# The low-rank first factors of the decay and the rate, taken from h and h shifted by one token, with the mixing vectors multiplied into the weights

## The chip, the cores and the metric

The kernel runs on one core of a Trainium2 chip. The metric is device time in microseconds (us) of one launch; lower is better. The core's engines work side by side, each through its own list of instructions in order: TensorE (PE in the profile, its weight loads PEld), VectorE (DVE), ScalarE (ACT), GpSimd (POOL), and SyncE (SP), which issues most of the DMAs. They wait for one another through semaphores.

## The reference

Two layers over 512 tokens of width 1024, in float32. Layer 0 is an RWKV-7 time mix and a SwiGLU FFN, layer 1 differential attention and an FFN. The change touches the time mix, which begins so (its scan over tokens and the rest of the model are left out):

```python
h_prev = jnp.pad(h, ((0, 0), (1, 0), (0, 0)))[:, :-1]
hh = h_prev - h
xr = h + hh * mu[0]
xw = h + hh * mu[1]
xk = h + hh * mu[2]
xv = h + hh * mu[3]
xa = h + hh * mu[4]
xg = h + hh * mu[5]
r = xr @ w_r
w = -jax.nn.softplus(-(w0 + jnp.tanh(xw @ w1) @ w2)) - 0.5
k = xk @ w_k
v = xv @ w_v
a = jax.nn.sigmoid(a0 + (xa @ a1) @ a2)
g = jax.nn.sigmoid(xg @ g1) @ g2
...
decay = jnp.exp(-jnp.exp(heads(w)))
```

`h` is the RMS-normalised input. `w1` and `a1` are 1024x64, `w2` and `a2` 64x1024, `w_r`, `w_k` and `w_v` 1024x1024.

## The kernel before, in words

Activations lie with features on the 128 partitions and the 512 tokens along the free dimension: eight tiles of 128 features make the width of 1024 (`KT` = 8; `kt` counts them). Precision comes from splitting a float32 operand into a rounded part (`hi`, type fp32r) and a rest (`lo`). `mm3` (lines 154 to 158) then makes one product of three fp32r matmuls (hi·hi, hi·lo, lo·hi). A plain float32 matmul stands in the trace as two instructions.

**The order.** Program order is written by generators, and a scheduler of the framework then sets the order on each engine. `merge` (line 99) deals out the steps of several generators in proportion to the numbers beside them. The first merge (line 480) has four: `normed` (eight steps that scale the input to h, line 452), two calls of `lora` (the first factors of decay and rate, tags `ca` and `cb`), and `r_half(0)`, the first half of r. After it come `rates` for half 0 (both second factors) and `k_half(0)`. Then `plan` (line 495) runs three streams: the recurrence's preparation and scan for heads 0 to 7, the remaining projections, and the same preparation for heads 8 to 15.

**A mix.** `mix_tile` (lines 366 to 374) makes one 128x512 tile of xr, xw and so on: ScalarE multiplies h by 1-mu (line 372), VectorE adds mu times h shifted by one token (line 373). Its default buffers are tag `xm`, of which there are two.

**Before the change.** `lora` loads a first factor twice side by side (line 381, so the 128 columns of the weight are w1 and w1 again), mixes a tile, and makes one float32 matmul of it per `kt` (line 392). `proj_p` (lines 187 to 206) makes r and k of half 0: per `kt` a mix, its cast to hi (line 199) and its rest (line 200), and twelve fp32r matmuls into four PSUM banks (tag `pj`); every second `kt` also a 512 KB weight load, its cast (line 195) and its rest (line 196). `lora2` multiplies the second factor: since the first result stands twice on the partitions, upper half as hi and lower half as lo (`halves`), a matmul over 128 rows (line 414) and one over 64 rows (line 415) make up the three products. `rates` calls it for decay and rate, eight banks per half, each evacuated by a sigmoid on ScalarE (line 538).

**Buffers** that matter: `wr` 3 (weights as loaded), `xm` 2, `xk` 9 (the mixes of k, kept for both halves), `pr` 7, `z` 6 (hi/lo pairs of `proj_p`), `s` 13, `pj` 4 banks, `ca` and `cb` 2 banks each.

**The end of a scan step.** `head_out` (line 879) normalises 128 tokens of eight heads, then turns them into feature order: four TensorE transposes into one bank (line 911), each followed by its ScalarE evacuation (line 912).

The functions that the change touches:

Of the kernel before, what the change touches and what calls it, by code (L numbers as in the profile page):

```python
# [34 lines left out]
VI = {n: i for i, n in enumerate(VECS)}  # L35
# [7 lines left out]
class Trunk:  # L43
# [3 lines left out]
                 gate=(172, 190, 1.0), out0=(190.5, 252.922016661, 1.25), pairs1=(65, 130, 1.0), solve1=(132.962208526, 188.90025602, 1.0))  # L47


    START = 8, 7.5, 7.5, 8  # L50


    RW = dict(s=13, z=6, b=2, xk=9, xm=2, pr=7, nv=3, it=1, u=2, rs=9, ho=4, ev=1, iv=1)
# [339 lines left out]
            yield  # L393
        out(*pss)

    def halves(self, dst, src):

        nc = self.nc
        nc.scalar.copy(dst, src)
        nc.vector.tensor_tensor(out=dst[C:P], in0=src[C:P], in1=dst[C:P].bitcast(F32), op=ALU.subtract)  # L400

    def lora2(self, x, W2, w, evac):

        nc = self.nc
        raw = self.T("wr", [P, 512])
        for f in (slice(0, C), slice(C, P)):
            nc.sync.dma_start(raw[f], W2[:, w * 512:w * 512 + 512])
        hi, lo = self.T("ho", [P, 512], F32R), self.T("ho", [P, 512], F32R)
        nc.scalar.copy(hi, raw)
        nc.vector.tensor_tensor(out=lo[0:C], in0=raw[0:C], in1=hi[0:C].bitcast(F32), op=ALU.subtract)  # L410
        for i in range(4):
            ps = self.bank()
            c = slice(i * P, i * P + P)
            nc.tensor.matmul(ps, hi[:, c], x, start=True, stop=False)
            nc.tensor.matmul(ps, lo[0:C, c], x[0:C], start=False, stop=True)
            evac(w * 4 + i, ps)

    def gate2(self, pg, w, evac):

# [18 lines left out]
    def rwkv(self, turn):  # L438
        nc, A = self.nc, self.A
# [7 lines left out]
        h = xT  # L447

        def normed():
            for j in range(KT):  # L450
                v = h[j // 2][:, j % 2, :]
                nc.vector.scalar_tensor_tensor(out=v, in0=v, scalar=self.vec("g_mix0", j), in1=bc, op0=ALU.mult, op1=ALU.mult)
                yield
# [4 lines left out]
        for p in range(NP):  # L458
            nc.vector.tensor_scalar(self.rkc[:, p, :], self.cst[:, C_BO:C_BO + 2], self.vec("r_k", p), None, op0=ALU.mult)
        self.lw = cp.tile([P, D], F32, name="lw")  # L460
        nc.sync.dma_start(self.lw, A["lnx_w"].broadcast_to([P, D]))
        self.v_d = self.dr.tile([2, 2, S, 4, C], F32, name="v_d")
        self.st_d = self.dr.tile([2, NCH, P, 4, 8 * C], F32, name="st_d")
        self.sel = cp.tile([P, NT, P], F32, name="sel")
        nc.gpsimd.dma_start(self.sel, A["sel"])
        self.R, self.Pt, self.kept = {}, {}, {}
        self.oT = {}

        pwa = []

        def low(i):
            def out(ps):
                pwa or pwa.append(self.T("s", [P, 2, S], F32R))
                if i:
                    return self.halves(pwa[0][:, 1, :], ps)
                t = self.T("pr", [P, S])
                nc.scalar.activation(t, ps, AF.Tanh)
                self.halves(pwa[0][:, 0, :], t)
            return out
        self.merge(*zip((normed(), self.lora(h, 1, [(A["w1"], 2)], low(0), "ca"), self.lora(h, 4, [(A["a1"], 2)], low(1), "cb"), self.r_half(0)),  # L480
                        self.START))
        sg, aa = self.rates(pwa[0], 0)
        kr, ld, pg, sa, x1 = ([], []), ([], []), [], [(sg, aa)], []
        self.drain(self.k_half(0, kr[0]))

        def rates():
            sa.append(self.rates(pwa[0], 1))
            yield

        def out(w):  # L490
# [3 lines left out]
        t = self.TIMES  # L494
# [12 lines left out]
    def mixes(self, key, m, w):  # L507

        kept = self.kept.setdefault(key, {})

        def mix(kt):
            if key == "r":
                return self.mix_tile(self.h, m, kt)
            if w:
                return kept.pop(kt)
            x = kept[kt] = self.mix_tile(self.h, m, kt, "xk")
            return x
        return mix
# [11 lines left out]
                nc.vector.tensor_tensor(out=lo[g], in0=v[g], in1=hi[g].bitcast(F32), op=ALU.subtract)  # L530
        return self.lora(self.h, 5, [(self.A["g1a"], 1), (self.A["g1b"], 3)], out, "pj")

    def rates(self, low, w):
        nc, A = self.nc, self.A
        sg = [self.T("s", [P, 2, S]) for _ in range(2)]
        aa = [self.T("s", [P, 2, S]) for _ in range(2)]
        for i, W2, dst, b in ((0, A["w2"], sg, "w0"), (1, A["a2"], aa, "a0")):
            self.lora2(low[:, i, :], W2, w, lambda o, ps: nc.scalar.activation(dst[o // 2 - 2 * w][:, o % 2, :], ps, AF.Sigmoid, bias=self.vec(b, o)))
        return sg, aa

    def r_half(self, w):
# [337 lines left out]
    def head_out(self, w, tt, y):  # L879
        nc = self.nc  # L880
# [21 lines left out]
        yo = sq.rearrange("p (a b) c -> p a b c", b=2)  # L902
# [4 lines left out]
        yield  # L907
        ps = self.bank("cb")
        for i in range(4):
            p = w4 + i  # L910
            nc.tensor.transpose(ps[:, i * P:(i + 1) * P], yo[:, i].rearrange("p a b -> p (a b)"), self.ident)
            nc.scalar.activation(self.oT[p // 2][:, p % 2, tt * P:(tt + 1) * P], ps[:, i * P:(i + 1) * P], AF.Identity, bias=self.vec("lnx_b", p))

    def ffn(self, xT, l, tag, out=None):
# [367 lines left out]
```

## Time and profile before

| | us |
|---|---|
| median of 3 runs | 1524.42 (1516.05 to 1524.76) |
| the profiled execution | 1518.63 |
| its span, first to last instruction | 1516.8 |
| PE busy | 1447.9 (95%) |
| VectorE busy | 787.3 (52%) |
| ScalarE busy | 529.1 (35%) |
| GpSimd busy | 187.3 (12%) |

The span has four parts: the load and normalisation of the input (to about 28 us), the time mix (to about 507 us), the first FFN and the attention, and the second FFN. A busy PE is not a PE at its peak: matmuls overlap, so the busy time of one is longer than the distance from one start to the next, and the latter is what a stream of them costs. The granted clock (PEclk) is that of TensorE, 1.00 being 2.4 GHz and 0.50 being 1.2 GHz.

### The profile page before, as it was taken

What the parts mean: (1) busy time and instruction counts of PE and PEld (TensorE: products, weight loads), DVE (VectorE), ACT (ScalarE), POOL (GpSimd) and SP (SyncE); (2) the same over time, 40 slices, a digit from 0 to 9 for tenths busy, and PEclk for the clock granted to TensorE, in tenths of its full rate; (3) what the DMA queues carried; (4) which work ended last, traced back from release to release, by engine and by line L of the source; (5) the groups of instructions that cost most, each with busy time, mean ns of one, the idle gap of its engine ahead of it and who ended that gap; (6) DMA issues with size and microseconds to landing.
All of it is one profiled execution on the core that took longest, in us unless ns stands there. A gap on an engine that the chain in (4) does not pass through costs nothing.

```text
span 1516.8 us, 23107 instructions
## 1 busy us (share of the span) xinstructions
PE 1447.9 (95%) x9576; PEld 1140.0 (75%) x9576; DVE 787.3 (52%) x1511; ACT 529.1 (35%) x926; POOL 187.3 (12%) x156
## 2 busy tenths in 40 slices
PE   3899999999997999999999989999999999999998
PEld 2465555767685788888888879988778888888887
DVE  6735549677666644433323276666665444443222
ACT  4652341213423433222222153556654323232111
POOL 0002313100000111111100023111001111111000
PEclk9989999999998999999999999999999999999999
DMA  5112423776321322222222222111112232322231
GB/s 159 57 69 93 165 105 107 281 241 207 133 89 42 116 96 85 98 97 97 96 93 96 95 92 84 59 68 43 42 43 97 96 99 92 102 91 100 98 122 64
DMA packets 59162, 155.82 MB, mean 103 GB/s; under 512 B 12848, under 2 KB 19248, under 8 KB 57008
## 3 DMA queue, kind: packets, MB, share of 16 engines
q1 hardware_dynamic: 57856, 152.76, 29.3%
q8 instruction: 75, 1.23, 0.3%
q10 hardware_dynamic: 1120, 1.32, 0.3%
q14 instruction: 31, 0.25, 0.1%
q0 software_dynamic: 80, 0.26, 0.0%
HBM read 133.34 MB, written 20.97 MB: 102 GB/s over the span
## 4 chain that ended last, share of the span: by engine, by line
PE 83%; DVE 9%; ACT 3%; POOL 2%; issue 1%; DMA 1%; ACTq 0%; POOLq 0%
PE pj L156 15%; PE pj L157 15%; PE pj L158 15%; PE pj L182 3%; PE pj L216 3%; PE d L1058 2%; PE cb L875 2%; PE d L1060 2%; PE d L1059 2%; PE ca L833 2%; PE cb L743 1%; PE a L1156 1%; PE ca L157 1%; PE cb L157 1%; PE ca L158 1%
## 5 line engine op out<-in xcount | busy, mean ns | idle before, releaser
L150 ACT CAST wh<-wr 128x1024 fp32r<-128x1024 f32 x153 | 160.8, 1051 | 498.4 <-PE pj L157 224.2
L151 DVE TENSOR_TENSOR wl<-wr,wh 128x1024 fp32r<-128x1024 f32 x153 | 187.0, 1223 | 183.7 <-ACT wh L150 182.0
L156 PE MATMUL pj<-xa,wh 128*128 128x512 f32 x352 | 139.2, 395 | 1.3 <-ACT wh L150 1.3
L157 PE MATMUL pj<-xa,wh 128*128 128x512 f32 x352 | 138.9, 395 | 0.0
L158 PE MATMUL pj<-xa,wl 128*128 128x512 f32 x352 | 138.8, 395 | 0.0
L156 PE MATMUL pj<-xb,wh 128*128 128x512 f32 x352 | 137.1, 389 | 0.0
L158 PE MATMUL pj<-xb,wl 128*128 128x512 f32 x352 | 137.0, 389 | 0.0
L157 PE MATMUL pj<-xb,wh 128*128 128x512 f32 x352 | 137.0, 389 | 0.0
L945 POOL TENSOR_TENSOR hid<-ev,hid 128x512 fp32r<-128x512 f32 x44 | 68.2, 1551 | 403.6 <-ACT hid L944 403.6
L941 DVE TENSOR_TENSOR ev<-pj,bc 128x512 f32<-128x512 f32 x44 | 30.4, 691 | 144.5 <-PE pj L158 144.5
L938 DVE TENSOR_TENSOR ev<-pj,bc 128x512 f32<-128x512 f32 x44 | 30.4, 692 | 117.0 <-PE pj L158 114.7
L156 PEld LDWEIGHTS pj<-xa,wh 128*128 128x128 f32 x352 | 66.3, 188 | 17.4 <-ACT wh L150 2.2
L158 PEld LDWEIGHTS pj<-xa,wl 128*128 128x128 f32 x352 | 66.3, 188 | 15.7
L157 PEld LDWEIGHTS pj<-xa,wh 128*128 128x128 f32 x352 | 66.3, 188 | 15.3
L157 PEld LDWEIGHTS pj<-xb,wh 128*128 128x128 f32 x352 | 66.1, 188 | 13.8
L156 PEld LDWEIGHTS pj<-xb,wh 128*128 128x128 f32 x352 | 66.1, 188 | 13.7
L158 PEld LDWEIGHTS pj<-xb,wl 128*128 128x128 f32 x352 | 66.1, 188 | 13.6
L158 PE MATMUL pj<-hid,wl 128*128 128x512 f32 x176 | 68.5, 389 | 0.0
L156 PE MATMUL pj<-hid,wh 128*128 128x512 f32 x176 | 68.5, 389 | 0.0
L157 PE MATMUL pj<-hid,wh 128*128 128x512 f32 x176 | 68.5, 389 | 0.0
L216 PE MATMUL pj<-wr,xk 128*128 128x512 f32 x128 | 63.5, 635 | 0.0
L227 POOL TENSOR_TENSOR ty<-ty,mhalf 128x8 f32<-128x8 f32 (+1 forms) x20 | 35.4, 1770 | 157.6 <-DVE ty L1094 125.7
(337 smaller groups left out, 3124.7 us busy)
## 6 DMA issues: line engine op xcount, KB each, us to landing
wr<-in_wgu SPq DMA_DIRECT2D x88, 512.0 KB, 3.5
wr<-in_wdn SPq DMA_DIRECT2D x44, 512.0 KB, 3.5
st_d<-z SPq DMA_DIRECT2D x16, 1024.0 KB, 4.7
z<-st_d SPq DMA_DIRECT2D x16, 1024.0 KB, 6.3
wr<-in_w_kv SPq DMA_DIRECT2D x16, 512.0 KB, 3.6
wr<-in_w_r SPq DMA_DIRECT2D x8, 512.0 KB, 3.5
wr<-in_w_k SPq DMA_DIRECT2D x8, 512.0 KB, 3.5
wr<-in_w_v SPq DMA_DIRECT2D x8, 512.0 KB, 3.8
```

The source lines that it names most:

```text
L150: nc.scalar.copy(hi, raw)
L151: nc.vector.tensor_tensor(out=lo, in0=raw, in1=hi.bitcast(F32), op=ALU.subtract)
L156: mm(out, wh, xh, start=start, stop=False)
L157: mm(out, wh, xl, start=False, stop=False)
L158: mm(out, wl, xh, start=False, stop=stop)
L182: self.nc.tensor.matmul(pss[i], w[:, kt % 2, i * P:i * P + P], x, start=kt == kts[0], stop=kt == kts[-1])
L216: self.nc.tensor.matmul(pss[tt], x[:, tt * P:(tt + 1) * P], w[:, kt % 2, :], start=kt == 0, stop=kt == KT - 1)
L227: nc.gpsimd.tensor_tensor(out=y, in0=m, in1=half.to_broadcast(shp), op=ALU.pow)
L833: nc.tensor.matmul(ps[f, i * C:(i + 1) * C], L(f, i), R[f, i, :], start=False, stop=n == len(parts) - 1 and i == 3)
L938: nc.vector.tensor_tensor(out=a, in0=pss[0], in1=bc, op=ALU.mult)
L941: nc.vector.tensor_tensor(out=b, in0=pss[1], in1=bc, op=ALU.mult)
L945: nc.gpsimd.tensor_tensor(out=t[:, 1, :], in0=b, in1=t[:, 0, :].bitcast(F32), op=ALU.subtract)
```

## The change

The two `lora` calls become one generator, `lora_h`, and the mixes of decay and rate go away. Since xw = (1-mu)·h + mu·h_prev, xw·w1 equals h·((1-mu)·w1) + h_prev·(mu·w1): the kernel loads w1 and a1 once each, side by side (64 columns each), multiplies both by 1-mu and by mu (four VectorE instructions on 128x8x64), and makes two float32 matmuls per `kt`, one of h and one of h shifted by a token (511 columns), into one bank for both. Rows 0 to 63 of the result are the decay's, 64 to 127 the rate's; Tanh runs on the first, a copy on the second, then one split makes hi and lo. `rates` loads w2 and a2 into the two halves of one tile, splits it once, and uses `mm3` over 64 rows: three matmuls for a bank instead of two. "Three changes" are also: r's mixes of half 0 use the seven `pr` buffers instead of the two `xm`; the loads of `lw` and `sel` stand later in the program; and `head_out` makes its four transposes ahead of the four evacuations.

```diff
-    START = 8, 7.5, 7.5, 8
+    START = 8, 7.5, 8
...
-    def halves(self, dst, src):
...
-    def lora2(self, x, W2, w, evac):
...
-        for i in range(4):
-            ps = self.bank()
-            c = slice(i * P, i * P + P)
-            nc.tensor.matmul(ps, hi[:, c], x, start=True, stop=False)
-            nc.tensor.matmul(ps, lo[0:C, c], x[0:C], start=False, stop=True)
-            evac(w * 4 + i, ps)
+    def lora_h(self, h, tag):
+        nc, A = self.nc, self.A
+        raw = self.T("wr", [P, KT, P])
+        W = [self.T("s", [P, KT, P]) for _ in range(2)]
+        for i, (m, n) in enumerate(((1, "w1"), (4, "a1"))):
+            c = slice(i * C, i * C + C)
+            nc.sync.dma_start(raw[:, :, c], A[n])
+            j = VI[f"mu{m}"] * KT
+            for t, f in zip(W, (self.omu[:, m * KT:(m + 1) * KT], self.par[:, j:j + KT])):
+                nc.vector.tensor_tensor(out=t[:, :, c], in0=raw[:, :, c], in1=f.unsqueeze(2).to_broadcast([P, KT, C]), op=ALU.mult)
+        ps = self.bank(tag)
+        mm = nc.tensor.matmul
+        for kt in range(KT):
+            x = h[kt // 2][:, kt % 2, :]
+            now = lambda: mm(ps, W[0][:, kt, :], x, start=kt == 0, stop=kt == KT - 1)
+            if kt == 0:
+                now()
+            mm(ps[:, 1:S], W[1][:, kt, :], x[:, 0:S - 1], start=False, stop=False)
+            if kt:
+                now()
+            yield
+        t = self.T("pr", [P, S])
+        nc.scalar.activation(t[0:C], ps[0:C], AF.Tanh)
+        nc.vector.tensor_copy(t[C:P], ps[C:P])
+        self.low = self.T("s", [P, 2, S], F32R)
+        nc.scalar.copy(self.low[:, 0, :], t)
+        nc.vector.tensor_tensor(out=self.low[:, 1, :], in0=t, in1=self.low[:, 0, :].bitcast(F32), op=ALU.subtract)
...
-        self.merge(*zip((normed(), self.lora(h, 1, [(A["w1"], 2)], low(0), "ca"), self.lora(h, 4, [(A["a1"], 2)], low(1), "cb"), self.r_half(0)),
-                        self.START))
-        sg, aa = self.rates(pwa[0], 0)
+        self.merge(*zip((normed(), self.lora_h(h, "ca"), self.r_half(0)), self.START))
+        sg, aa = self.rates(0)
...
-                return self.mix_tile(self.h, m, kt)
+                return self.mix_tile(self.h, m, kt, "xm" if w else "pr")
...
-    def rates(self, low, w):
+    def rates(self, w):
...
+        raw = self.T("wr", [P, 512])
+        F = slice(0, C), slice(C, P)
+        for f, n in zip(F, ("w2", "a2")):
+            nc.sync.dma_start(raw[f], A[n][:, w * 512:w * 512 + 512])
+        hi, lo = self.T("ho", [P, 512], F32R), self.T("ho", [P, 512], F32R)
+        nc.scalar.copy(hi, raw)
+        nc.vector.tensor_tensor(out=lo, in0=raw, in1=hi.bitcast(F32), op=ALU.subtract)
+        for f, dst, b in zip(F, (sg, aa), ("w0", "a0")):
+            for i in range(4):
+                ps = self.bank()
+                c = slice(i * P, i * P + P)
+                self.mm3(ps, hi[f, c], lo[f, c], self.low[f, 0, :], self.low[f, 1, :], True, True)
+                nc.scalar.activation(dst[i // 2][:, i % 2, :], ps, AF.Sigmoid, bias=self.vec(b, w * 4 + i))
...
         for i in range(4):
+            nc.tensor.transpose(ps[:, i * P:(i + 1) * P], yo[:, i].rearrange("p a b -> p (a b)"), self.ident)
+        for i in range(4):
             p = w4 + i
-            nc.tensor.transpose(ps[:, i * P:(i + 1) * P], yo[:, i].rearrange("p a b -> p (a b)"), self.ident)
             nc.scalar.activation(self.oT[p // 2][:, p % 2, tt * P:(tt + 1) * P], ps[:, i * P:(i + 1) * P], AF.Identity, bias=self.vec("lnx_b", p))
```

Outside the time mix the order on the engines stays. In it, the scheduler's order moves at three places that matter below. The first is VectorE at the end of the input's norm, from the reciprocal root (its last steps write `rstd`; `ty` are small tiles) to the first scaling of x into h. Before:

```order
L229 TENSOR_TENSOR ty_127<-ty_125 128x4
L979 SCALAR_TENSOR_TENSOR hcol<-hcol,cst 128x1
L230 SCALAR_TENSOR_TENSOR ty_127<-ty_127,ty_122 128x4
L231 SCALAR_TENSOR_TENSOR rstd_124<-ty_127,ty_125 128x4
L1000 TENSOR_SCALAR sgn<-sgn 128x1
L253 TENSOR_SCALAR pr_132<-cst,rstd_124 128x128
```

Now, with `s_192` and `s_193` the two weight tiles of `lora_h` and `wr_191` the loaded w1 and a1:

```order
L229 TENSOR_TENSOR ty_127<-ty_125 128x4
L407 TENSOR_TENSOR s_192<-wr_191,omu 128x8x64
L230 SCALAR_TENSOR_TENSOR ty_127<-ty_127,ty_122 128x4
L407 TENSOR_TENSOR s_193<-wr_191,par 128x8x64
L231 SCALAR_TENSOR_TENSOR rstd_124<-ty_127,ty_125 128x4
L407 TENSOR_TENSOR s_192<-wr_191,omu 128x8x64
L253 TENSOR_SCALAR pr_132<-cst,rstd_124 128x128
L407 TENSOR_TENSOR s_193<-wr_191,par 128x8x64
```

Three of the four weight multiplications stand between the steps of the reciprocal root, in place of one-column instructions that move behind them; the fourth stands behind the instructions of line 253.

The second is ScalarE from the last evacuation of r to the sigmoids (`pr` takes Tanh's output, `s_413` and `s_368` the split first factor, `z` the pairs of k). Before:

```order
L545 COPY s_164<-pj_169 128x512
L199 CAST z_479<-xk_482 128x512
L477 ACTIVATE pr_414<-ca_196 128x512
L199 CAST z_479<-xk_499 128x512
L399 CAST s_413<-pr_414 128x512
L399 CAST s_413<-cb_204 128x512
L195 CAST z_518<-wr_516 128x1024
L538 ACT_TABLE_LOAD
```

Now:

```order
L553 COPY s_162<-pj_167 128x512
L195 CAST z_511<-wr_509 128x1024
L199 CAST z_512<-xk_515 128x512
L420 ACTIVATE pr_365<-ca_200 64x512
L199 CAST z_512<-xk_532 128x512
L423 CAST s_368<-pr_365 128x512
L546 ACT_TABLE_LOAD
```

A 128x1024 weight cast moves from behind the split to a place ahead of Tanh. On VectorE the subtraction that ends the split (line 424) stands behind line 196 of the same pair, the copy of the rate's rows (line 421) and two instructions of line 200.

The third is PE at the same point. Before, the last two first-factor matmuls are followed by `lora2`'s pairs of a 128-row and a 64-row matmul:

```order
L392 MATMUL ca_196<-xm_405,wr_193 128x512
L392 MATMUL cb_204<-xm_409,wr_201 128x512
L414 MATMUL pj_431<-s_413,ho_427 128x512
L415 MATMUL pj_431<-s_413,ho_428 128x512
L414 MATMUL pj_435<-s_413,ho_427 128x512
```

Now:

```order
L415 MATMUL ca_200<-x_70,s_193 128x511
L412 MATMUL ca_200<-x_70,s_192 128x512
L156 MATMUL pj_382<-s_368,ho_378 128x512
L156 MATMUL pj_387<-s_368,ho_378 128x512
L156 MATMUL pj_392<-s_368,ho_378 128x512
L156 MATMUL pj_397<-s_368,ho_378 128x512
L157 MATMUL pj_382<-s_368,ho_378 128x512
L158 MATMUL pj_382<-s_368,ho_379 128x512
```

The first-factor matmuls read the tiles of h themselves, and all 24 matmuls of the second factors are over 64 rows, twelve on rows 0 to 63 and then twelve on rows 64 to 127. At the start of the stage three of the sixteen first-factor matmuls stand ahead of r's first.

On SP, w1 and a1 are each issued once instead of twice, the second w_r load follows them at once, and `lw` stands behind that; w2 and a2 are issued once each.

## Rows read from the trace of the kernel before

**Rows 1.** Busy time by stretch. The columns are the stretch and its length in us, then for PE, PEld, DVE, ACT and POOL busy us and (x instructions), the granted clock, the DMA share and GB/s.

```profile
9.00:13.40 4.40, 0.00 (x0) 0.00 (x0) 2.55 (x5) 1.20 (x3) 0.00 (x0) 1.00 1.03 355
...
41.00:75.40 34.40, 28.61 (x96) 17.51 (x96) 23.90 (x34) 21.22 (x34) 0.00 (x0) 1.00 0.19 59
77.40:80.40 3.00, 2.95 (x7) 1.29 (x7) 1.92 (x2) 2.97 (x5) 0.00 (x0) 1.00 0.63 253
80.40:90.50 10.10, 10.10 (x19) 5.33 (x19) 2.08 (x3) 6.89 (x12) 0.00 (x0) 0.51 0.13 50
```

**Rows 2.** Timeline of PE in two rounds of that stage: start us, busy us (modelled, longer than the distance to the next start), instruction; in brackets idle time before it.

```profile
61.26 1.02 PE L392 MATMUL ca<-xm,wr 128*128 128x512 f32 x2
62.12 1.02 PE L392 MATMUL cb<-xm,wr 128*128 128x512 f32 x2
64.53 1.19 PE L156 MATMUL pj<-z,z 128*128 128x512 f32 x4 [1.39 <-ACT z L199]
65.56 0.39 PE L157 MATMUL pj<-z,z 128*128 128x512 f32 x1
65.79 0.39 PE L158 MATMUL pj<-z,z 128*128 128x512 f32 x1
70.68 1.19 PE L156 MATMUL pj<-z,z 128*128 128x512 f32 x4 [1.39 <-ACT z L199]
```

**Rows 3.** Groups of instructions by line from 28.5 to 75.4 us: busy us, mean ns of one, idle before.

```profile
L373 DVE SCALAR_TENSOR_TENSOR xm<-x,par,xm 128x511 f32<-128x511 f32 x22 | 16.4, 749 | 9.0 <-ACT xm L372 8.5
L372 ACT ACTIVATE xm<-x,omu 128x512 f32<-128x512 f32 x22 | 15.8, 720 | 13.5 <-PE ca L392 10.6 <-DVE z L200 1.5 <-PE cb L392 0.7
L199 ACT CAST z<-xm 128x512 fp32r<-128x512 f32 x8 | 4.9, 616 | 1.1 <-DVE xm L373 1.1
L200 DVE TENSOR_TENSOR z<-xm,z 128x512 fp32r<-128x512 f32 x8 | 5.5, 684 | 0.0
L156 PEld LDWEIGHTS pj<-z,z 128*128 128x128 f32 x32 | 6.0, 201 | 13.6 <-ACT z L199 11.7 <-issue 1.0
```

**Rows 4.** Timeline of VectorE in the input's norm.

```profile
13.35 0.69 DVE L265 TENSOR_TENSOR pr<-x 128x512 f32<-128x512 f32 x1 [1.60 <-DMA x<-in_xT]
...
25.07 1.41 DVE L452 SCALAR_TENSOR_TENSOR x<-x,par,cb 128x512 f32<-128x512 f32 x2 [1.58 <-PE cb L254]
```

**Rows 5.** DMA issues of SP in the first 30 us: start us, us in the queue, number of issues.

```profile
13.34 1.37 SPq L381 DMA_DIRECT2D wr<-in_a  x2
```

**Rows 6.** DMAs of the first 60 us, grouped: KB each, median us from issue to landing.

```profile
lw<-in_lnx_w SPq DMA_DIRECT2D x1, 512.0 KB, 9.8
wr<-in_a SPq DMA_DIRECT2D x2, 256.0 KB, 4.4
```

**Rows 7.** Timeline of PE at r's first matmuls.

```profile
31.24 0.63 PE L158 MATMUL pj<-z,z 128*128 128x512 f32 x1
31.66 0.63 PE L156 MATMUL pj<-z,z 128*128 128x512 f32 x1
```

**Rows 8.** Timeline of PE around the second factors of half 0 and the first half of k.

```profile
74.42 1.02 PE L392 MATMUL cb<-xm,wr 128*128 128x512 f32 x2
77.45 0.51 PE L414 MATMUL pj<-s,ho 128*128 128x512 f32 x1 [2.01 <-DVE s L400]
77.89 0.49 PE L415 MATMUL pj<-s,ho 64*128 64x512 f32 x1
...
86.91 0.79 PE L156 MATMUL pj<-z,z 128*128 128x512 f32 x1
...
110.61 0.59 PE L182 MATMUL pj<-xm,wr 128*128 128x512 f32 x1
```

**Rows 9.** Groups of ScalarE's instructions by line from 75 to 110 us: busy us, mean ns of one, idle before.

```profile
L538 ACT ACTIVATE s<-pj,par 128x512 f32<-128x512 f32 x8 | 5.3, 687 | 3.2 <-PE pj L415 3.2
L195 ACT CAST z<-wr 128x1024 fp32r<-128x1024 f32 x3 | 3.2, 1063 | 2.5 <-PE pj L158 2.5
L399 ACT CAST s<-pr 128x512 fp32r<-128x512 f32 x1 | 0.7, 660 | 0.0
L477 ACT ACTIVATE pr<-ca 128x512 f32<-128x512 f32 x1 | 0.6, 632 | 0.0
```

**Rows 10.** Timeline of PE around the second factors of half 1.

```profile
207.02 0.79 PE L414 MATMUL pj<-s,ho 128*128 128x512 f32 x1
...
210.74 1.95 PE L589 MATMUL cb<-cst,pr 128*128 128x2 f32 x16
...
217.49 4.74 PE L216 MATMUL pj<-wr,xk 128*128 128x512 f32 x7
```

**Rows 11.** Busy time by stretch (columns as in rows 1), one stretch with a short fall of the clock and one at the end of the second factors of half 1.

```profile
250.00:260.00 10.00, 9.17 (x75) 5.54 (x72) 9.78 (x21) 1.51 (x3) 3.06 (x4) 0.83 0.57 201
...
217.50:220.50 3.00, 3.00 (x5) 1.45 (x5) 0.39 (x1) 2.88 (x4) 0.28 (x1) 0.50 0.00 0
```

**Rows 12.** PE's waits from 110.6 to 507 us (who waited for whom, us in total, times, longest us), and below them, from the view of line 911, its durations (ns min/median/max) and the idle time of PE and its weight loads together before it until line 912 was done (us, times).

```profile
PE cb L911 <- ACT s L912: 1.4, 3, 0.5
...
L911 PE MATMUL cb<-cst,ho x32: 270/328/475, 345.9 to 479.9; 128*128 128x128 f32 x32
...
  ACT s L912: 4.9, 11
```

**Rows 13.** Timeline of PE: eight instructions in a row over 8 of the 128 rows.

```profile
147.73 1.15 PE L718 MATMUL cb<-it,sel 8*128 8x128 f32 x8
```

More of the change, by code (lines that the diff above doesn't have):

```diff
@@ L394, in lora @@
         out(*pss)
-    def halves(self, dst, src):
-        nc = self.nc
-        nc.scalar.copy(dst, src)
-        nc.vector.tensor_tensor(out=dst[C:P], in0=src[C:P], in1=dst[C:P].bitcast(F32), op=ALU.subtract)
-    def lora2(self, x, W2, w, evac):
[L404 to L410, printed above, removed]
-        for i in range(4):
-            ps = self.bank()
-            c = slice(i * P, i * P + P)
-            nc.tensor.matmul(ps, hi[:, c], x, start=True, stop=False)
-            nc.tensor.matmul(ps, lo[0:C, c], x[0:C], start=False, stop=True)
-            evac(w * 4 + i, ps)
+    def lora_h(self, h, tag):
[25 more added lines that the diff above has]
+        nc.vector.tensor_tensor(out=self.low[:, 1, :], in0=t, in1=self.low[:, 0, :].bitcast(F32), op=ALU.subtract)
     def gate2(self, pg, w, evac):
@@ L460, in rwkv @@
         self.lw = cp.tile([P, D], F32, name="lw")
-        nc.sync.dma_start(self.lw, A["lnx_w"].broadcast_to([P, D]))
         self.v_d = self.dr.tile([2, 2, S, 4, C], F32, name="v_d")
@@ L464, in rwkv @@
         self.sel = cp.tile([P, NT, P], F32, name="sel")
-        nc.gpsimd.dma_start(self.sel, A["sel"])
         self.R, self.Pt, self.kept = {}, {}, {}
         self.oT = {}
[L469 to L479, printed above, removed]
-        self.merge(*zip((normed(), self.lora(h, 1, [(A["w1"], 2)], low(0), "ca"), self.lora(h, 4, [(A["a1"], 2)], low(1), "cb"), self.r_half(0)),
-                        self.START))
-        sg, aa = self.rates(pwa[0], 0)
+        self.merge(*zip((normed(), self.lora_h(h, "ca"), self.r_half(0)), self.START))
+        sg, aa = self.rates(0)
         kr, ld, pg, sa, x1 = ([], []), ([], []), [], [(sg, aa)], []
+        nc.gpsimd.dma_start(self.sel, A["sel"])
         self.drain(self.k_half(0, kr[0]))
+        nc.sync.dma_start(self.lw, A["lnx_w"].broadcast_to([P, D]))
         def rates():
-            sa.append(self.rates(pwa[0], 1))
+            sa.append(self.rates(1))
             yield
@@ L536, in rates @@
         aa = [self.T("s", [P, 2, S]) for _ in range(2)]
-        for i, W2, dst, b in ((0, A["w2"], sg, "w0"), (1, A["a2"], aa, "a0")):
-            self.lora2(low[:, i, :], W2, w, lambda o, ps: nc.scalar.activation(dst[o // 2 - 2 * w][:, o % 2, :], ps, AF.Sigmoid, bias=self.vec(b, o)))
+        raw = self.T("wr", [P, 512])
[11 more added lines that the diff above has]
+                nc.scalar.activation(dst[i // 2][:, i % 2, :], ps, AF.Sigmoid, bias=self.vec(b, w * 4 + i))
         return sg, aa
```

## The prediction

> **What bounds the kernel now.** I read the busy time by stretch first. Away from the start PE is busy nearly all the time, so a change pays only where PE waits, runs at the lower clock, or gets less to do. From 41 to 75.4 us, where r's first half runs beside the first factors, PE is busy 28.61 of 34.40 us [rows 1]. The PE timeline shows a round that repeats every 6.15 us (64.53 to 70.68), with 1.39 us idle before line 156 in each [rows 2]. A round holds twelve fp32r matmuls, 0.23 us from one start to the next, and two float32 ones at 0.86 (61.26 to 62.12): 2.75 + 1.72 = 4.47 us of work. The missing 1.68 us is a loop through two `xm` buffers: three mixes per round share them, so the next mix waits until line 392 has read one, 10.6 us in all [rows 3], and only behind two mixes and a cast can PE go on. Next comes the handover: 2.0 us idle, then the second factors from 77.45 to 86.91, at 0.43 to 0.44 us a matmul at first (77.45 to 77.89), because a matmul over 128 rows and one over 64 alternate [rows 8]. Three us into that, the granted clock falls from 1.00 to 0.51 (1.2 GHz) until 90.5, in the middle of k [rows 1].
>
> **Part A, r and the first factors.** The start: two things oppose each other. `lw` (512 KB) leaves the queue ahead of w_r, w1 and a1, which halve in bytes (two loads of 256 KB instead of four [rows 6]), so the last input tile, which lands at 13.35 [rows 4], may come earlier; 512 KB at the 355 GB/s that the DMAs moved from 9 to 13.4 us [rows 1] is 1.4 us, and since other loads move up behind it I take 1.2. Instead three weight multiplications stand in the reciprocal root's chain; the nearest row is a 128x512 VectorE subtraction, 0.68 us [rows 3], three times 2.0; the one-column instructions that leave give a little back, +1.8 taken. The fourth hides in the 1.58 us for which VectorE waits before line 452 [rows 4]. Scaling of x thus starts at 25.07 - 1.2 + 1.8 = 25.7; bounds 23.7 (no cost) and 28 (no DMA gain, and w1 and a1 push the last tile back by another us). a1 landed at 13.34 + 4.4 = 17.7 [rows 5, 6], before that root was done, and goes out earlier now, so the product does not wait for it.
>
> PE needs one scaled tile (0.7 us), no mix: it starts at 26.4. Its work until r ends is 16 x 0.86 + 96 x 0.228 = 13.8 + 21.9 = 35.7 us. Before, r's first matmuls came 0.42 apart (31.24 to 31.66) [rows 7] and not 0.23; I charge some 4 us at such half speed again, +2.1. So r and the first factors end at 64.2 if PE is fed. It is: a round now needs of ScalarE one mix (0.72), one cast (0.62), half a weight cast (0.53) and one kept mix of k (0.72), 2.6 us; of VectorE the same mixes (2 x 0.75), one rest (0.68), half a weight rest (as much again) and at first a scaling (0.7), 3.6 us, both below 4.47 [rows 3, 9]. r's mixes have seven buffers, and those of decay and rate are gone (16 on each engine). Before, the stage ended at 74.42 + 0.86 = 75.3 [rows 8]: **-11.1 us**, bounds -5.5 (half of it comes back) and -13.
>
> **Part B, handover, second factors, first half of k.** Behind the last first-factor matmul ScalarE may still be at a weight cast and one of k's (1.06 + 0.6, begun when r's last matmul is through, 1.7 before the end), then Tanh 0.63, a cast 0.6, the split 0.66 [rows 9]: PE starts about 2.4 us after the end, and waits 0.4 more for VectorE's rest, 2.8 instead of 2.15: +0.7. All 24 matmuls are then over 64 rows without alternation. No row shows such a stream of fp32r. Nearest: 128 rows without alternation, 0.228 [rows 2]; the alternating pairs, 0.43 [rows 8]. Eight-row matmuls in a row take 1.15 us for eight 128-column passes of float32, 0.14 each, against 0.11 if their loads cost nothing (a quarter of 0.43) and 0.29 if a load of 0.19 [rows 3] ran before each [rows 13]. So I take 0.228: 5.5 us instead of 9.46, -4.0. A sigmoid takes 0.69 [rows 9], as long as a bank's three matmuls. The clock: it fell after 2 us without work and 3 us of thin work, and here there are 2.8 us without. I charge one fall as short as the shortest I found, 0.83 over 10 us, that is 3.4 us at half [rows 11]: +1.7, bounds 0 and 5 (10.1 us as before). k's first half has 96 x 0.228 = 21.9 us of work and took 110.61 - 86.91 = 23.7, its beginning at the low clock [rows 1, 8]: -1.8. Sum **-3.4 us**, bounds +1.5 and -6.
>
> **Part C, second factors of half 1.** They take 217.49 - 207.02 = 10.47 us less 1.9 for line 589 between them: 8.6, and three us of half speed follow (1.5 lost) [rows 10, 11]. Now 5.5, and I charge a short fall again (1.7), since line 589 stays: **-2.9**, bounds 0 and -4.6. ScalarE's sigmoids and evacuations there could hold it back: -2.5 taken.
>
> **Part D, the transposes.** PE waits 1.4 us for line 912 between transposes, and PE's sequencers together 4.9 [rows 12]; that goes. Against it, three transposes (0.33 each, overlapped) move up ahead of the scan's next matmuls, eight times: 8 us if every one stood in the chain. I take **-1.5**, nearest the wait that PE itself shows, bounds +8 and -4.9. The moved `lw` and `sel` have their use after 130 us: nothing, unless the start is late by that much. The second factor's single load and split take one VectorE and one ScalarE instruction per half away, off the path.
>
> Behind 110 us the work and its order are the same and PE is the engine that waits least, so what is won is kept. Sum: -11.1 - 3.4 - 2.5 - 1.5 = -18.5. Against the profiled execution's 1518.63: 1500.1. That execution lies 5.8 below the median of 1524.42 (the runs spread from 1516.05 to 1524.76); the same difference from the median gives 1505.9. I predict **1502**, between the two.
>
> **Rivals.** *The 64-row stream does not overlap.* At 0.43 each, the second factors take 10.3 us instead of 5.5, twice: 9.6 lost, 1502 + 10 = **1512**. For: the alternating pairs do just that. Against: the eight-row matmuls. The Trainium skill, "TensorE: Matmul & The Clock Gate", Part 3, says that weight loads overlap running matmuls only when the row group differs; by that rule twelve matmuls in a row on rows 0 to 63 would be serial, with this rival's sum. The trace disagrees for 128 rows, where loads of 0.19 us vanish in 0.228; it shows no such stream over 64. Chance 12%.
>
> *PE is not fed in part A.* If a chain through ScalarE and VectorE still costs 0.7 us in each of the eight rounds (of 1.68 now), 5.6 come back: **1508**. For: both are busy over 60% there now [rows 1]. Against: the sums per round above. 10%.
>
> *Slower.* The clock falls in the longer wait and stays at 1.2 GHz through the 64-row matmuls and k: their 27.4 us of work take 54.8. From part B's forecast this is 27.4 - 1.7 = 25.7 more: **1528**, and slower than before. It decides once over 41 us run at half speed (20 us lost). For: the clock fell just there [rows 1]. Against: it came back within 4 us of a dense stream's start at 86.91. 4%.
>
> *More.* No fall of the clock at either place, and the scan gains by grouped transposes: 3.4 + 3.5 more, **1495**. 9%.
>
> **Numbers.** My forecast has 65%. About 1% (15.2 us) is what a measurement can tell from no change; faster by more than that is below 1509.2. The forecast's own spread (part bounds, and the runs' spread of 9 us) reaches from 1494 to 1512; with the first rival the range is **1492 to 1514**. Below 1509.2 lie 55 of the forecast's 65%, all 9 of the last rival, 6 of the second and 2 of the first: faster 0.72. Slower by more than 1% (above 1539.7) would be only the slow clock together with another loss: 0.03. Same: 0.25.
>
> **What would show it.** In the profile of the changed kernel: rounds of 4.5 us without idle before line 156 and the last first-factor matmul near 64 us (A); 24 matmuls within about 6 us, k ending near 95 (B); lines 156 to 158 over 64 rows 0.23 apart, not 0.43 (first rival); the granted clock between 64 and 95. I am wrong if the weight multiplications wait for w1 or a1, if rounds stay above 5 us, or if the 15 us won by 110 us are not there any more at 507.

## The result, and the profile after

The changed kernel takes 1503.8 us (median of 4 runs, 1503.17 to 1508.46) where the kernel before, run beside it, took 1524.51: a ratio of 0.989, with a 95% interval of 0.9858 to 0.9921. That is 12 to 22 us faster, and the forecast was 1502. The profiled execution took 1504.01 us (span 1502.2), 14.6 less than the profiled one of before; the medians differ by 20.7, because before's own runs spread over 9 us (1516.05 to 1524.76) and the profiled one lies 5.9 below their median.

The first view is the busy time by stretch of the changed kernel (columns as in rows 1).

```profile
26.30:64.70 38.40, 38.35 (x128) 24.95 (x128) 30.99 (x44) 26.88 (x43) 0.00 (x0) 1.00 0.24 86
64.70:67.30 2.60, 0.13 (x1) 0.00 (x0) 2.53 (x3) 2.10 (x4) 0.00 (x0) 1.00 0.04 6
...
69.00:79.30 10.30, 10.30 (x29) 7.84 (x27) 0.00 (x0) 5.28 (x8) 0.00 (x0) 0.50 0.00 0
79.30:99.30 20.00, 20.00 (x90) 16.52 (x89) 4.65 (x6) 3.91 (x7) 0.00 (x0) 1.00 0.08 27
...
202.20:208.80 6.60, 6.60 (x12) 3.56 (x12) 3.68 (x6) 5.03 (x7) 2.19 (x1) 0.50 0.00 0
```

In r's half with the first factors PE is busy 38.35 of 38.40 us, where it had been busy 28.61 of 34.40 [rows 1]. Then it waits 2.6 us. But the granted clock falls for 10.3 us at the second factors of half 0, and for 6.6 us at those of half 1: the first as long as before [rows 1], not short as the forecast had it.

The second view is the timeline of PE: the starts of two rounds of r and the first factors, the last of the first factors, the second factors of half 0, k's first matmul, the first matmul behind k, then second factors of half 1 at either level of the clock, and the first matmul behind them. The row marked PEld is the weight load of the matmul that starts at 196.76.

```profile
46.42 0.80 PE L156 MATMUL pj<-z,z 128*128 128x512 f32 x1
...
50.88 0.80 PE L156 MATMUL pj<-z,z 128*128 128x512 f32 x1
...
63.81 1.02 PE L412 MATMUL ca<-x,s 128*128 128x512 f32 x2
67.36 1.19 PE L156 MATMUL pj<-s,ho 64*128 64x512 f32 x4 [2.54 <-ACT s L423]
...
75.78 0.79 PE L156 MATMUL pj<-z,z 128*128 128x512 f32 x1
...
99.29 3.60 PE L182 MATMUL pj<-xm,wr 128*128 128x512 f32 x8
...
196.53 0.39 PE L157 MATMUL pj<-s,ho 64*128 64x512 f32 x1
196.53 0.18 PEld L158 LDWEIGHTS pj<-s,ho 64*128 64x128 f32 x1
196.76 0.39 PE L158 MATMUL pj<-s,ho 64*128 64x512 f32 x1
...
204.53 0.62 PE L157 MATMUL pj<-s,ho 64*128 64x512 f32 x1
204.95 0.62 PE L158 MATMUL pj<-s,ho 64*128 64x512 f32 x1
205.51 5.38 PE L216 MATMUL pj<-wr,xk 128*128 128x512 f32 x8
```

A round takes 4.46 us (46.42 to 50.88) instead of 6.15 [rows 2]. Matmuls over 64 rows come 0.23 us apart at the full clock (196.53 to 196.76) and 0.42 at half (204.53 to 204.95); the 0.18 us load of the second runs beside the first. From such timelines comes the balance: when the same piece of work starts, or where it says so ends, in both kernels.

| place on PE | before | after | difference |
|---|---|---|---|
| end of the first factors | 75.28 | 64.67 | -10.6 |
| second factors, half 0 | 77.45 | 67.36 | -10.1 |
| k, first half | 86.91 | 75.78 | -11.1 |
| first matmul behind it | 110.61 | 99.29 | -11.3 |
| second factors, half 1 | 207.02 | 196.19 | -10.8 |
| first matmul behind them | 217.49 | 205.51 | -12.0 |
| scan, first matmul | 289.15 | 277.65 | -11.5 |
| scan, end of its last matmul | 468.39 | 452.44 | -16.0 |
| output projection behind it | 484.38 | 469.91 | -14.5 |
| end of the span | 1516.8 | 1502.2 | -14.6 |

The scan itself became 4.5 us shorter, and the stretch from its end to the output projection 1.5 longer (16.0, then 17.5). The last group of the transposes (line 918 now, 911 before) stands in that stretch; first the row from the timeline of PE, then the durations of that line, then the releaser of the projection:

```profile
462.10 1.08 PE L918 MATMUL cb<-cst,ho 128*128 128x128 f32 x4 [5.54 <-DVE ho L914]
...
L918 PE MATMUL cb<-cst,ho x32: 271/273/444, 334.8 to 462.8; 128*128 128x128 f32 x32
...
469.91 0.79 PE L156 MATMUL pj<-s,s 128*128 128x512 f32 x1 [6.73 <-ACT s L670]
```

The transposes' median went from 328 to 273 ns, and the idle time of 4.9 us until an evacuation was done [rows 12] is no longer among the waits of line 918.

The start is read from VectorE's timeline:

```profile
12.40 0.69 DVE L265 TENSOR_TENSOR pr<-x 128x512 f32<-128x512 f32 x1 [0.60 <-DMA x<-in_xT]
...
21.07 0.16 DVE L229 TENSOR_TENSOR ty<-ty 128x4 f32<-128x4 f32 x1 [0.94 <-POOL ty L227]
21.15 0.69 DVE L407 TENSOR_TENSOR s<-wr,omu 128x512 f32<-128x512 f32 x1
...
25.55 2.06 DVE L460 SCALAR_TENSOR_TENSOR x<-x,par,cb 128x512 f32<-128x512 f32 x3 [0.66 <-PE cb L254]
```

The last input tile is used 0.95 us earlier than before [rows 4], the weight multiplications (line 407) stand between the steps of the reciprocal root as forecast, and the scaling of x begins at 25.55 us instead of 25.07.

### The profile page after: what moved, and what is told of

It reads as the page before. It is cut to its first block, busy times and chain, and to the rows that moved or that the text cites. A ratio compares the mean times of both kernels' runs of the same rounds, so it can differ in the third digit from the quotient of the medians.

```text
span 1502.2 us, 23112 instructions
## 1 busy us (share of the span) xinstructions
PE 1438.6 (96%) x9592; PEld 1142.1 (76%) x9592; DVE 775.7 (52%) x1497; ACT 514.0 (34%) x907; POOL 188.6 (13%) x156
## 4 chain that ended last, share of the span: by engine, by line
PE 83%; DVE 9%; ACT 3%; POOL 2%; issue 2%; DMA 1%; ACTq 0%; POOLq 0%
PE pj L156 15%; PE pj L157 15%; PE pj L158 15%; PE pj L182 3%; PE pj L216 3%; PE d L1067 2%; PE cb L883 2%; PE d L1069 2%; PE d L1068 2%; PE ca L841 2%; PE cb L751 1%; PE a L1165 1%; PE ca L157 1%; PE cb L157 1%; PE ca L156 1%
## 5 line engine op out<-in xcount | busy, mean ns | idle before, releaser
L156 PEld LDWEIGHTS pj<-xa,wh 128*128 128x128 f32 x352 | 66.3, 188 | 17.5 <-ACT wh L150 2.2
```

What stands on the lines that cost most here:

```text
L156: mm(out, wh, xh, start=start, stop=False)
```

## The experiments

### Part A: the loop through two buffers

```diff
 # kernel before
 def mix(kt):
     if key == "r":
-        return self.mix_tile(self.h, m, kt)
+        return self.mix_tile(self.h, m, kt, "xm" if w else "pr")
```

> The kernel before with one part of the change: r's mixes of half 0 take their tiles from the seven `pr` buffers, everything else as before. Theory (part A of the prediction: a loop through two `xm` buffers costs 1.68 us in each round): decay and rate now have a buffer each, the loop is open, a round takes about 4.5 us instead of 6.15, the stage ends near 65 us instead of 75.3, and the kernel takes 8 to 10 us less than before. Rival (the mixing itself is the limit, since three mixes a round are still made): VectorE and ScalarE need some 4.4 us a round and hold PE up, rounds of 5 us or more, at most 5 us won. If the theory holds, moving the mixing vectors into the weights is worth nothing in this stage by itself.

It took 1513.38 us against 1524.2 beside it, a ratio of 0.9939 (0.9921 to 0.9956). Its PE timeline at three starts of line 392, and the busy time of a stretch inside the stage:

```profile
47.53 1.02 PE L392 MATMUL ca<-xm,wr 128*128 128x512 f32 x2
...
52.02 1.02 PE L392 MATMUL ca<-xm,wr 128*128 128x512 f32 x2
...
56.51 1.02 PE L392 MATMUL ca<-xm,wr 128*128 128x512 f32 x2
...
41.00:66.00 25.00, 25.00 (x92) 17.00 (x91) 24.10 (x36) 19.66 (x32) 0.00 (x0) 1.00 0.25 79
```

Rounds of 4.49 us with PE busy throughout: the loop is open, and the stage ends at 67.2 us, 8.1 earlier than before. VectorE, busy 24.10 of 25 us, is just quick enough, so the rival was close but did not come. Of the 10.6 us of part A, 8.1 are thus to be had by another tag alone, at the end of this stage. Not all of that stays: the clock's fall at the second factors lasts 13.6 us here (71.7 to 85.3) against 10.1 before, k is through 5.9 us earlier than before (104.67 against 110.61), and the profiled span is 5.1 shorter (1511.7). Of the other 2.5 us nearly all belongs to the start: here PE's first first-factor matmul is at 28.60 us, in the changed kernel at 26.35, since it needs no mix.

```diff
 # changed kernel
-        return self.mix_tile(self.h, m, kt, "xm" if w else "pr")
+        return self.mix_tile(self.h, m, kt)
```

> The changed kernel with r's mixes back in the two `xm` buffers. Theory: with decay's and rate's mixes gone only one mix a round uses them, and it is read by ScalarE and VectorE alone, so two buffers suffice: rounds stay at 4.46 us, the time within 1 us of the changed kernel. Rival (the buffers were needed): idle before line 156 comes back, up to 1 us a round, 4 to 8 us more.

The stage ends at 63.87 us with rounds of 4.46, and the kernel takes 1505.73 us, a ratio to before of 0.989 (0.9868 to 0.9912), the same as the changed kernel's. The median lies 1.9 us above the changed kernel's, where 1 was expected, but the runs of the two overlap (1503.26 to 1508.63 here). The theory holds: with the mixes of decay and rate gone, r needs no more buffers. The change carries two remedies for one loop, and either opens it.

```diff
 # changed kernel
+        nc.sync.dma_start(self.lw, A["lnx_w"].broadcast_to([P, D]))
         self.v_d = ...
 ...
         self.drain(self.k_half(0, kr[0]))
-        nc.sync.dma_start(self.lw, A["lnx_w"].broadcast_to([P, D]))
```

> The changed kernel with the load of `lw` in its old place in the program, ahead of the first-factor and r weights. Theory (its 512 KB ahead of the others are why the last input tile is used at 13.35 us before and at 12.40 now): the last tile comes 0.9 to 1.4 us later, PE's first matmul of the first factors at 27.3 to 27.8 instead of 26.35, and the same shift at 99 us. Rival (the smaller loads of w1 and a1 make the difference): last tile at 12.4 still, nothing moves.

One row each of VectorE's and of PE's timeline:

```profile
13.74 0.69 DVE L265 TENSOR_TENSOR pr<-x 128x512 f32<-128x512 f32 x1 [1.92 <-DMA x<-in_xT]
...
27.69 2.08 PE L412 MATMUL ca<-x,s 128*128 128x512 f32 x2 [0.84 <-DVE x L460]
```

The last tile is used 1.34 us later than in the changed kernel, and so is PE's first matmul: the theory holds, by the load's place in the queue. But of the 1.34 us only 0.7 are left behind k (99.97 against 99.29), where the same shift was expected, and nothing at the scan's first matmul (277.64 against 277.65). In the whole, 1506.19 us with a ratio of 0.9902 (0.9871 to 0.9934), it can't be told from the changed kernel.

### Parts B and C: why the clock falls, and for how long

```diff
 # changed kernel
-    START = 8, 7.5, 8
+    START = 10, 9.5, 8
```

> The changed kernel with the first factors merged a step and a half ahead of r (10, 9.5, 8 in place of 8, 7.5, 8 steps), so that Tanh and the split run beside r's last two rounds. Both theories expect PE's wait before the second factors, 2.54 us, to shrink under 1 us. Theory (the wait is what lets the clock fall at 69 us, for 10.3 us): the clock stays at 1.00 or falls for much less, the second factors take 5.5 us instead of 8.4 and k 22 instead of 23.5, 6 to 7 us less than the changed kernel. Rival (the matmuls over 64 rows make it fall, as at 202 us, where PE did not wait before them): the clock falls for 10 us again, and only the wait is won, 1.5 to 2.5 us.

It took 1502.36 us, a ratio of 0.9868 (0.9848 to 0.9888). Busy time by stretch from the last first factor through the second factors and k:

```profile
56.00:62.80 6.80, 6.10 (x25) 4.17 (x23) 4.71 (x7) 4.18 (x9) 0.00 (x0) 1.00 0.23 77
62.80:68.30 5.50, 4.73 (x20) 3.51 (x20) 1.23 (x1) 5.47 (x9) 0.00 (x0) 1.00 0.25 70
68.30:75.40 7.10, 7.10 (x18) 5.09 (x18) 1.29 (x2) 3.54 (x7) 0.00 (x0) 0.52 0.05 20
```

Of the wait 0.70 us is left ahead of r's last round and 0.77 between the second factors, but the clock falls all the same, 5.5 us after the first matmul over 64 rows, and stays at half for some 6.8 us (a mean of 0.52 over 7.1). So far this is the rival: the wait is not needed for a fall, though without it the fall is shorter than the rival's 10 us. k is through at 94.68 us, 4.6 earlier than in the changed kernel. Of that 2.2 is an earlier start (first factors from 24.17 us): the loads of w1 and a1 now stand ahead of both loads of w_r, and the last input tile, used at 10.75 us, gains by it. Of the 4.6 us only 1.8 are left at the output projection (468.12); this trace has two falls of the clock on the way that the changed kernel's lacks, 3.3 us or a little more at 0.50 from 269.8 and from 375.6 us.

The next edit keeps the wait and takes away the 64 rows:

```diff
 # changed kernel, rates()
-        hi, lo = self.T("ho", [P, 512], F32R), self.T("ho", [P, 512], F32R)
-        nc.scalar.copy(hi, raw)
-        nc.vector.tensor_tensor(out=lo, in0=raw, in1=hi.bitcast(F32), op=ALU.subtract)
-        for f, dst, b in zip(F, (sg, aa), ("w0", "a0")):
+        Z = []
+        for f, g in zip(F, F[::-1]):
+            hi, lo = self.T("ho", [P, 512], F32R), self.T("ho", [P, 512], F32R)
+            nc.gpsimd.memset(hi.bitcast(F32)[g], 0.0)
+            nc.gpsimd.memset(lo.bitcast(F32)[g], 0.0)
+            nc.scalar.copy(hi[f], raw[f])
+            nc.vector.tensor_tensor(out=lo[f], in0=raw[f], in1=hi[f].bitcast(F32), op=ALU.subtract)
+            Z.append((hi, lo))
+        for (hi, lo), dst, b in zip(Z, (sg, aa), ("w0", "a0")):
 ...
-                self.mm3(ps, hi[f, c], lo[f, c], self.low[f, 0, :], self.low[f, 1, :], True, True)
+                self.mm3(ps, hi[:, c], lo[:, c], self.low[:, 0, :], self.low[:, 1, :], True, True)
```

> The changed kernel with the 24 second-factor matmuls of each half over all 128 rows: decay's and rate's weights stand in tiles of their own whose other 64 rows are zero, and the moving operand is the whole stacked first result. Same number of matmuls, same columns, two more casts and rests of 64 rows and four memsets a half. Theory (matmuls over 64 rows let the clock fall): no fall at 202 us in half 1, 3 to 3.5 us won there; in half 0, where PE still waits 2.5 us ahead of them, the fall stays or starts later. Rival (the fall of half 1 comes from line 597, 128x2 columns, or from what runs before): both falls as in the changed kernel, 0 to 1 us more for the added casts.

It took 1499.15 us, a ratio of 0.9854 (0.9821 to 0.9887). The wait, the second factors of half 0 in three pieces, and those of half 1:

```profile
63.50:66.30 2.80, 0.17 (x2) 0.04 (x1) 2.70 (x4) 2.28 (x6) 0.00 (x0) 1.00 0.19 25
66.30:67.40 1.10, 1.10 (x4) 0.73 (x4) 1.10 (x2) 1.10 (x1) 0.00 (x0) 0.75 0.89 335
67.40:70.60 3.20, 3.20 (x10) 2.50 (x9) 0.02 (x1) 1.58 (x4) 0.00 (x0) 0.55 0.07 27
70.60:73.40 2.80, 2.80 (x14) 2.32 (x13) 0.00 (x0) 2.80 (x5) 0.99 (x2) 1.00 0.00 0
...
193.20:201.00 7.80, 7.80 (x43) 6.48 (x42) 2.41 (x8) 7.06 (x11) 0.00 (x0) 1.00 0.18 67
```

In half 1 the fall is gone: 7.8 us at 1.00, though the 128x2 matmuls of line 597 (602 in this kernel) stand between the second factors as before. In half 0 it still comes behind the wait, but the clock is back after some 3.4 us (half of the second stretch, with 0.75, and nine tenths of the third, with 0.55), while second factors are still running. With both causes out:

```diff
 # kernel of the last experiment
-    START = 8, 7.5, 8
+    START = 10, 9.5, 8
```

> The same with the first factors merged a step and a half ahead of r, so that neither the long wait nor the matmuls over 64 rows are left in half 0. Theory (either of the two is enough to let the clock fall, and without both it stays): granted clock 1.00 from 60 to 95 us, k ends 3 to 3.5 us earlier than with the first factors ahead alone (94.68). Rival (neither matters, something else in the stretch does): a fall of 7 to 10 us between 65 and 80 us again.

```profile
56.90:63.60 6.70, 6.00 (x25) 4.35 (x24) 4.64 (x7) 4.10 (x9) 0.00 (x0) 1.00 0.23 78
63.60:70.40 6.80, 5.76 (x25) 4.43 (x24) 1.23 (x1) 6.77 (x11) 0.98 (x2) 1.00 0.25 77
70.40:92.20 21.80, 21.80 (x98) 18.04 (x97) 5.95 (x8) 6.03 (x11) 0.99 (x2) 1.00 0.08 25
...
188.10:196.00 7.90, 7.90 (x43) 6.57 (x42) 2.50 (x8) 7.16 (x11) 0.00 (x0) 1.00 0.19 66
```

No fall at either place, although PE waits 0.7 and 1.0 us in the first two stretches. k is through at 92.18 us, 2.5 earlier than with the first factors ahead alone: the second factors begin 0.75 later (63.61 against 62.86), and from there to k's end it takes 3.25 less. The 3 to 3.5 that were expected at k's end come from that part; the later start takes 0.75 of it back. The kernel takes 1494.95 us, a ratio of 0.9825 (0.9797 to 0.9852), and beats both. The four kernels together, with the time that PE spent at 1.2 GHz:

| ahead of the second factors of half 0 | over 64 rows | over 128 rows |
|---|---|---|
| PE waits 2.5 to 2.6 us | for 10.3 us | for 3.4 us |
| no wait above 1.04 us | for some 6.8 us | not at all |

### Part D: the transposes

```diff
 # changed kernel, head_out
         for i in range(4):
             nc.tensor.transpose(ps[:, i * P:(i + 1) * P], ...)
-        for i in range(4):
             p = w4 + i
             nc.scalar.activation(self.oT[p // 2][:, p % 2, ...], ps[:, i * P:(i + 1) * P], ...)
```

> The changed kernel with each transpose of `head_out` followed by its evacuation again, as before. Theory (the scan's gain of 4.4 us, of which 1.5 went again behind its end, comes from the grouped transposes): the scan's last matmuls come 3 to 4 us later, and the time is 2 to 4 us above the changed kernel. Rival (the scan was shorter because its inputs were ready earlier): within 1 us of the changed kernel.

The scan from its first to its last matmul takes 178.25 us (277.58 to 455.83) against 174.79, and the stretch behind it 15.8 against 17.5, as the theory has it. But the median was 1509.14 us, while its profiled execution took 1504.72. The next two runs time both kernels again, side by side:

> The changed kernel itself, beside the next three on the same chip, as the measure for them: within 3 us of 1503.8, with the clock's falls at 69 and 202 us again. If these falls come and go from run to run, no place of theirs can be charged to a part of the change.

> The changed kernel with each transpose of `head_out` followed by its evacuation, timed again. The first run had the scan's last matmul 3.4 us later, 1.76 of it left at the output projection, 0.7 at the end of the profiled execution, but a median 5 us above. Theory (what its places show is what it costs): 1 to 2.5 us above the changed kernel run beside it. Rival (the median was right): 4 to 6 us.

The changed kernel took 1504.81 us (1503.53 to 1506.18; ratio 0.9891, 0.9874 to 0.9909), with the clock's falls at both places again, the other 1508.89 (1506.34 to 1509.31; ratio 0.9917, 0.9902 to 0.9932): 4.1 us more, with no run of either inside the range of the other's. That is the rival's size, as far as medians go. In the profiled executions of the two the difference is 3.65 us at the output projection (471.01 and 474.66), and it arises so: 1.7 up to line 216 at 205 us, 1.2 from there to the scan, 2.3 in the scan, and -1.5 behind it. Up to the scan both kernels issue the same work in the same order, and the trace shows what differs there: in this execution of the second kernel the clock's falls at the two places of second factors last some 3.4 us longer each than in the changed kernel's (10.1 and 6.7 us); in return it lacks a short fall behind k, at 105 us.

```profile
67.10:80.60 13.50, 13.50 (x35) 10.00 (x35) 0.44 (x1) 5.75 (x9) 0.00 (x0) 0.50 0.04 16
...
200.20:210.30 10.10, 10.10 (x23) 6.37 (x24) 3.68 (x6) 5.99 (x9) 2.19 (x1) 0.50 0.00 0
```

Where the transposes stand, the two pairs of executions give 0.8 and 1.8 us. All thirteen profiled executions of this document give a firmer figure: the four with single transposes take 178.12 to 179.24 us for the scan and 15.8 to 16.0 for the stretch behind it, the nine with grouped ones 173.97 to 175.84 and 17.5 (16.9 where only the last group is undone). That is 3.6 us won on average and 1.5 lost, about 2.1 in all. The medians agree once the clock is taken out: span times mean granted clock is 1479.1 us on average over the nine executions of the changed kernel and 1481.3 over the ten of this one, a difference of 2.2, where the mean spans differ by 3.6; the rest goes with a lower clock. So the theory's size is the better one, and why the clock falls longer in some executions than in others stays open.

```diff
 # changed kernel, head_out
+        def back(i):
+            p = w4 + i
+            nc.scalar.activation(self.oT[p // 2][:, p % 2, ...], ps[:, i * P:(i + 1) * P], ...)
+        last = w and tt == NT - 1
         for i in range(4):
             nc.tensor.transpose(ps[:, i * P:(i + 1) * P], ...)
-        for i in range(4):
-            p = w4 + i
-            nc.scalar.activation(self.oT[p // 2][:, p % 2, ...], ps[:, i * P:(i + 1) * P], ...)
+            if last:
+                back(i)
+        for i in range(0 if last else 4):
+            back(i)
```

> The changed kernel with the transposes grouped everywhere but in the last `head_out`, which has no matmuls left to stand beside. Theory (the four evacuations in a row hold up ScalarE's casts for the output projection, so the stretch from the scan's last matmul to that projection went from 16.0 to 17.5 us): that stretch goes back to 15.8 to 16, the scan keeps its gain, 1.5 us less than the changed kernel. Rival (that stretch hangs on the weight cast of line 670, not on the evacuations): 17.5 us again, no gain.

1504.33 us, a ratio of 0.9896 (0.9878 to 0.9913): the same as the changed kernel within the noise. The stretch took 16.9 us, 0.6 of the 1.5 us back. ScalarE's timeline there:

```profile
453.78 1.14 ACT L919 ACTIVATE s<-cb,par 128x128 f32<-128x128 f32 x4 [2.12 <-PE cb L922]
454.80 0.65 ACT L896 ACTIVATE ho<-ho 128x512 f32<-128x512 f32 x1
461.40 0.37 ACT L919 ACTIVATE s<-cb,par 128x128 f32<-128x128 f32 x1 [5.96 <-PE cb L922]
```

From the end of the last transpose to the projection it is 4.0 us again, as before the change (464.16 to 468.17; before 480.38 to 484.38). But the last group but one also falls into this stretch, and its four evacuations stand in a row ahead of line 896, the square that starts the last norm's chain. That square comes 3.5 us behind the scan's end here and in the changed kernel, and 2.6 before the change, which is the other 0.9 us. The theory named the right engine and one of two places.

> The changed kernel with the second factors over 128 rows, the first factors a step and a half ahead, and the last transposes one by one. Theory (the three gains stand in different stretches and add up): 1494.95 less 1.5, between 1492 and 1495. Rival (VectorE bounds the stretch from 210 to 270 us, and what PE wins ahead of it or behind is lost there or to the clock): 1495 to 1498.

1494.98 us, a ratio of 0.983 (0.9813 to 0.9848): nothing beyond the 1494.95 without the last edit. It had k's end as early (92.07) and the scan's last matmul 2.1 us later (444.95 against 442.81). Two stretches behind the second factors of half 1, and one inside the scan:

```profile
210.00:240.00 30.00, 27.86 (x203) 16.48 (x203) 28.96 (x58) 4.66 (x9) 10.91 (x11) 1.00 0.33 114
240.00:269.50 29.50, 26.88 (x484) 19.78 (x482) 20.34 (x37) 7.18 (x14) 5.95 (x8) 0.88 0.62 217
...
369.90:373.20 3.30, 3.30 (x18) 2.54 (x13) 2.81 (x5) 1.32 (x3) 0.00 (x0) 0.50 0.01 4
```

From 210 to 240 us VectorE is busy 28.96 of 30, PE 27.86; without the last edit it is 28.97 and 27.85, so the rival's bound through VectorE is there, but it is the same in both. After that the clock stands at 0.88, without the last edit at 0.94, as the rival's second part has it, yet the scan begins only 0.7 us later (269.47 against 268.79). Most of the 2.1 us, 1.5, arises in the scan itself, where the clock falls from 369.9 us, as it does not without the last edit. What brings that fall was not tried. Behind the scan 0.6 us are won, as in the run before.

## Why the prediction was right, and where not

**Right: the loop of part A.** Forecast -11.1, measured -10.6; stage end forecast 64.2 and measured 64.67 us, rounds 4.5 and 4.46, PE's start 26.4 and 26.35. The cause, two buffers for three mixes, is shown by the kernel that changes the buffers alone, and by the one that changes all but them. The step did not see that those buffers by themselves bring 8.1 us, and that the new first factors then add little more than an earlier start. Inside the start both terms were too large, by 0.25 and 0.4 in opposite directions: input tile -0.95 (forecast -1.2), multiplications +1.4 (the chain from the mean of squares to the scaling took 6.84 us against 5.42; forecast +1.8).

**Right: the 64-row stream overlaps.** 0.23 us a matmul at the full clock, as taken from the 128-row stream; the first rival (0.43) did not come. The Trainium skill, "TensorE: Matmul & The Clock Gate", Part 3, has the loads overlap only when the row group differs; twelve matmuls in a row on the same 64 rows at 0.23 us apart, each with a 0.18 us load of its own beside the matmul ahead of it, do not agree with it. The 0.43 us between matmuls in half 0 of the changed kernel (68.98 us and after) stand where the clock is at 0.50.

**Wrong: the size of the clock's fall in part B.** The step that failed is the charge of "one fall as short as the shortest I found", 3.4 us at half and +1.7. It lasted 10.3 us, 5.15 lost, so the second factors took 8.4 us (67.36 to 75.78) instead of 5.5 and a slow beginning, and k kept its slow start and took 23.5 us, not 21.9. Part B brought 0.7 us instead of 3.4, which lies inside the step's bounds; its sign of k ending near 95 us failed, as k ends at 99.29. A short fall, 3.4 us, is what a stream over 128 rows shows behind the same wait; over 64 rows the price was that of the second factors before, 10.1 us [rows 1], which stood in the step as its upper bound and was the nearer row. The *slower* rival (all of k at 1.2 GHz) did not come, since the clock was back 3.5 us into k.

**Wrong in the same way: part C.** -1.2 instead of -2.5. A short fall was charged and 6.6 us came, shown to be the 64 rows' own: over 128 rows it is gone. The trace of before had a fall as long at this place, of which the step read only the three us behind the last matmul [rows 11]:

```profile
213.70:220.40 6.70, 6.70 (x10) 2.79 (x10) 3.68 (x6) 4.63 (x7) 2.19 (x1) 0.50 0.00 0
```

**Part D: the size right, its parts not.** Forecast -1.5. Between the two kernels the scan gained 4.5 and the stretch behind it lost 1.5, a net of 2.95; over all the profiled executions grouping gives 3.6 in the scan and costs 1.5 behind it, a net of 2.1. One reason why the two traces differ by more: that of before has a fall of the clock inside the scan (3.3 us at 0.50 from 391.2), that of the changed kernel has none. The scan's share is nearer to the 4.9 us of PE's sequencers than to the 1.4 that I took it from [rows 12], and that grouping costs something where ScalarE's next work stands behind it was in no term. The two misses cancel, which is luck.

**The sum.** By places: -10.6, -0.7, -1.2, -2.95, and +1.0 lost in two stretches between, which gives -14.5 against a forecast of -18.5 from the profiled execution. The time of 1502 came within 2 us partly by luck: the sum alone gave 1500.1, nearly 4 us too low, and the step up to 1502, made because the median of before lies above its profiled execution, happened to give half of that back. "What is won is kept" held to 1 us here, but not in every kernel: of 1.34 us at the start nothing was left at the scan, of 4.6 us at k's end 1.8 at the projection, and falls of the clock that come in one execution and not in another are part of it.

## What to carry to other kernels

When PE idles once per round, look for the tile that several mixes share before making the mixes cheaper: in part A another tag for one of them gave, at the end of the stage, three quarters of what the whole change gave there. A small matmul stage is not priced by its columns alone: if it uses half of the rows, look at the granted clock in it and behind it, and try zero rows that make it full. After a gain early in the program, compare the start of the same work at several places in both traces; each stretch with another limit can take part of the gain back.

## What was not expected of the hardware

The 24 fp32r matmuls over 64 of 128 rows, 0.23 us apart and with no wait above 0.8, were followed by a granted clock of 0.50 to 0.52 for 6.6 us or more in all eight profiled executions that have them in half 1 (at 202.2 us in the changed kernel), and in half 0 with the first factors ahead (at 68.3 us). The same number over 128 rows, half of them against zeros, kept 1.00 in half 1 in all three executions that have them. Behind a wait of 2.6 us, matmuls over 128 rows ran 3.4 us at half speed. Half of the rows does not always bring the clock down: in the scan, where over 2,000 of the 2,627 matmuls in the changed kernel's trace are smaller ones over 64 rows, with 128x512 ones in between, it kept 1.00.

```profile
277.60:452.40 174.80, 171.33 (x2627) 130.29 (x2624) 125.78 (x324) 45.99 (x100) 12.39 (x18) 1.00 0.51 172
```

What makes the difference was not tried. The mean granted clock of the span went from 0.985 in the changed kernel to 0.991 in the kernel of 1494.95 us, with no fewer matmuls.
